# Down projection with seven products for eight in 8 of its 22 contracted tiles, and two modulation blocks summed earlier

## The chip, the cores and the metric

One Trainium2 chip, one of its cores. The time is the device time of the whole program in microseconds (us); below it is the median of several runs. The engines are named as the profile names them: PE (TensorE matmuls), PEld (its weight loads), DVE (VectorE), ACT (ScalarE), POOL (GpSimd), SP (SyncE, which issues most DMAs).

## The reference

One layer of a streaming encoder for 512 + 64 tokens, model width 1024, feed-forward width 2816, all in float32. What matters here is its end, the feed-forward part, and the modulation vectors that feed it:

```python
mod = (jax.nn.silu(c) @ w_ada + b_ada)[:, None, :]
sh1, sc1, gt1, sh2, sc2, gt2 = jnp.split(mod, 6, axis=-1)
...
x = x + gt1 * mixed
h2 = rms_normalize(x) * g_norm_ffn * (1.0 + sc2) + sh2
gate, up = jnp.split(h2 @ w_gate_up, 2, axis=-1)
x = x + gt2 * ((jax.nn.silu(gate) * up) @ w_down)
```

`w_gate_up` is 1024 x 5632, `w_down` 2816 x 1024. `mod` has 6 x 1024 columns, which the kernel makes in 12 blocks of 512; the last two, u = 10 and 11, are `gt2`.

## The kernel before

**Numbers in two parts.** A float32 operand is split into a rounded high part (`...h`, type fp32r, by ACT) and the remainder as low part (`...l`, by DVE: value minus high part). A product is then three matmuls into one PSUM bank: high x high, high x low, low x high. The 576 tokens are two halves of TH = 288; a matmul has a 128 x 128 weight tile and 288 or 290 columns.

**The planner.** The code does not issue instructions. It records them; `Plan.order` then sorts them by a list schedule with durations of its own and a priority for each (the place in the code, moved by `R.prio`: 4000 is earlier, -2000 later), and the chip gets a fixed order for each engine. All instructions therefore carry one line, L573, and are told apart by their tiles.

**Gate and up products.** The hidden dimension has 22 tiles f. For f = 0, 1 four plain products per half are made. From f = 2 on, `STRASSEN` takes a 2 x 2 block scheme with seven products in place of eight: contraction in two halves of four tiles, `g` and `u` as the two column blocks (quadrants `B11`, `B21` in `raw`, `B12`, `B22` in `rawu`), the two token halves as the two row blocks. Operands of the tokens are `A11`, `A12`, `A22` and the sums `S1` to `S4` (tiles `xh...`, `xl...`), those of the weights `B11`, `B21`, `B22` and the sums `T1` to `T4` that DVE makes. The order of the products is 7, 6, 2, 5, then product 1 of the next tile, 3, 4. `prepare` splits the weights of a product into one of six buffers (`wh`, `wl`, three each), six products ahead. Three banks `x`, `y`, `z` collect the products; `evacuate` reads them between the products (tiles `t1`, `u2`, `v`, `gg`, `uu`), and `finish` applies the gate.

**Down projection.** `split_f` splits each finished tile f into `fh`, `fl`: three of them early, 19 at the turn from one projection to the other, mostly in the freed buffers of `A11` to `S4`. Then for each of eight column blocks a the whole contraction runs plainly: 22 tiles x 3 matmuls x 2 halves = 132 matmuls (`fm_in`), then the update of the residual (`x2r`, two DVE instructions per half, 256 and 32 wide), six transposes, copies and stores. For a = 7 the halves run one after the other.

**Modulation blocks 10 and 11.** `ada_columns` makes them during the first columns of the down projection: eight 128 x 512 pieces of `w_ada`, and on DVE for each piece two instructions that multiply it by a per-partition scalar and add it to an accumulator (`aacc`), so 32 for both blocks. Small matmuls with `pick` and a transpose then turn the sums into columns.

Of the kernel before, what the change touches and what calls it, by code (L numbers as in the profile page):

```python
# [13 lines left out]
P = 128  # L14
# [566 lines left out]
def build(tc, I, O):  # L581
# [227 lines left out]

    def ada_out(u, p):  # L810
        ra = adp.tile([P, P], F32, name=f"ra{u}", tag="ra", bufs=2)
        vec.tensor_copy(ra, p[:, 0:P])
        p2 = px(f"padt{u}", "py")
        pe.transpose(p2[:, 0:P], ra, ident)
        vec.tensor_tensor(modc[:, u // 2, 4 * (u % 2):4 * (u % 2) + 4, :],
                          p2[:, 0:P].rearrange("p (g s) -> p g s", g=4)[:, :, 0:2],
                          badc[:, 4 * u:4 * u + 4, None].to_broadcast([P, 4, 2]), OP.add)

    def ada_columns(u, pl, bufs, sums=("aacc0", "aacc1"), raws=None):
# [13 lines left out]
        p = px(f"padc{u}")  # L833
        R.slack = 3.0
        with R.prio(4000):
            for s in range(2):
                for g in range(4):
                    pe.matmul(p[32 * g:32 * g + 32, 0:P], pick[:, s], acc[s][:, P * g:P * g + P], start=(s == 0), stop=(s == 1),
                              tile_position=(0, 32 * g))
            ada_out(u, p)  # L840
        R.slack = SLACK
# [969 lines left out]
    def weight_sum(f, q):

        if (f, q) not in sums:
            b = rawf[f]
            x, y = {"T1": ("B12", "B11"), "T2": ("B22", "T1"), "T3": ("B22", "B12"), "T4": ("B21", "T2")}[q]
            y = b[y] if y in b else weight_sum(f, y)
            t = ffw.tile([P, 4, P], F32, name=f"{q}_{f}", tag=q, bufs=2 if q in ("T1", "T2") else 1)
            vec.tensor_tensor(t, b[x], y, OP.subtract)
# [3 lines left out]
    def prepare():  # L1822
        j = made[0]
        f, q = preps[j]
        pl, tag, bufs = (x2p, "wx", 2) if 6 <= j < NP0 else (wp, ("wh", "wl")[j % 2], NWH)
        wops[f, q] = t = pl.tile([P, 8, P], F32R, name=f"wf{j}", tag=tag, bufs=bufs)
        src = rawf[f][q] if q[0] == "B" else weight_sum(f, q)
        act.activation(t[:, 0:4], src, AF.Copy)
        vec.tensor_tensor(t[:, 4:8], src, t[:, 0:4].bitcast(F32), OP.subtract)
        left[f] -= 1  # L1830
        if left[f] == 0 and f + 2 < NFT:
            load_f(f + 2)
        made[0] += 1

    def product(f, w, x, out, starts):
        w = wops[f, w]
        n = TH if x in ("A21", "A22", "S1", "S3") else TW
        out = out[:, :n]
        for k in range(4):
            xh, xl = xqh[x, k // 2][:, k % 2, :n], xql[x, k // 2][:, k % 2, :n]  # L1840
            for a, m in ((k, xh), (k, xl), (4 + k, xh)):
                pe.matmul(out, w[:, a], m, start=(starts and k == 0 and a < 4 and m is xh), stop=(k == 3 and a == 7),
                          skip_group_check=not starts)

    fe = R.mkpool("fearly", side="right", reuse_waits="tile")
    NEARLY = 3
    fh = [fe.tile([P, T], F32R, name=f"fh{k}") for k in range(NEARLY)]
    fl_ = [fe.tile([P, T], F32R, name=f"fl{k}") for k in range(NEARLY)]
    ev = R.mkpool("evac", side="right", reuse_waits="tile")
    fa, banks, parts = [], {}, {}  # L1850

    def split_f(k):
        act.activation(fh[k], fa[k], AF.Copy)
        vec.tensor_tensor(fl_[k], fa[k], fh[k].bitcast(F32), OP.subtract)

    def part(f, n):
        d = parts.setdefault(f, {})
        if n not in d:
            d[n] = ev.tile([P, 2, TW] if n in ("gg", "uu") else [P, TW], F32, name=f"{n}{f}", tag=n, bufs=2)
        return d[n]  # L1860
# [29 lines left out]
    def bank(f, b):  # L1890
        if (f, b) not in banks:
# [11 lines left out]
    def free_after(j):  # L1903

        return -1 if j < NP0 else N0 // 2 + j - NP0 if j < NP0 + 6 else N0 + j - 6 - NP0

    load_f(0)
    load_f(1)
    for i, (f, w, x, b, starts, *p) in enumerate(steps):
# [11 lines left out]
        else:  # L1921
            with R.prio(4000):
                evacuate(f, p[0])
            if p[0] == 4 and f <= NEARLY + 1:
                split_f(f - 2)
        if i == N0 - 1:
            R.close(x2p)
            gp = R.mkpool("act", side="right", reuse_waits="tile")
            fa += [gp.tile([P, T], F32, name=f"f{k}") for k in range(NFT)]
            for k in range(NPLAIN):  # L1930
                finish(k)
    R.close(ffw)
    down_specs()
    fhl = R.mkpool("fhl", reuse_waits="tile")
    homes = [(q, j) for q in ("A11", "S3", "S2", "A12", "S1", "S4", "A22") for j in range(2)]
    for k in range(NEARLY, NFT):
        for d, n in ((fh, "h"), (fl_, "l")):
            if homes:
                d.append(fp.tile([P, T], F32R, name=f"f{n}{k}", tag=f"x{n}{homes[0][0]}{homes[0][1]}"))
            else:  # L1940
                d.append(fhl.tile([P, T], F32R, name=f"f{n}{k}"))
        homes = homes[1:]
    for k in range(NEARLY, NFT):
        split_f(k)
    R.close(gp, ev)
    adg = R.mkpool("adag", reuse_waits="tile")
    with R.prio(2000):
        for u in (10, 11):
            ada_columns(u, adg, 2)
        vec.tensor_scalar(gt2h, gt2, 0.5, None, op0=OP.mult)  # L1950
    yop = R.mkpool("yout", reuse_waits="tile")
    fd = (lambda k: fh[k], lambda k: fl_[k])
    for a in range(8):
        w = getw()
        xo = yop.tile([P, 2, TH], F32, name=f"x2r{a}", tag="x2r", bufs=3)
        sync.dma_start(xo, x2_d[:, a])
        yo = yop.tile([P, 6, P], F32, name=f"yo{a}", tag="yo", bufs=3)
        pss = [pmm(f"pwd{a}{hf}")[:, 0:1] for hf in range(2)] if a == 7 else None
        ps = None if pss else pmm(f"pwd{a}")
        if a < 7:  # L1960
            fm_in(ps, w, *fd)
        cols = slice(a * P, (a + 1) * P)
        if a < 2:
            c = yop.tile([P, 2, TH], F32, name=f"c{a}", tag="c", bufs=2)
            with R.prio(4000):
                act.activation(c, ps[:, :, :TH], AF.Copy)
            ps = c
        for hf in range(2):
            if a == 7:
                fm_one(pss[hf][:, 0, :TH], w, *fd, hf)  # L1970
            x = xo[:, hf]
            for s, c0, n in SEG:
                vec.scalar_tensor_tensor(x[:, c0:c0 + n], (pss[hf][:, 0] if pss else ps[:, hf])[:, c0:c0 + n], gt2h[:, a, s:s + 1], x[:, c0:c0 + n], op0=OP.mult, op1=OP.add)
            p = px(f"pyt{a}{hf}", ("px", "py")[hf])
            R.slack = 2.0 if a < 2 else SLACK
            for j, (c0, n) in enumerate(BLOCKS):
                pe.transpose(p[:n, j * P:(j + 1) * P], x[:, c0:c0 + n], ident)
            R.slack = SLACK
            act.activation(yo[:, 3 * hf], p[:, :P], AF.Copy)
            vec.tensor_copy(yo[:, 3 * hf + 1], p[:, P:2 * P])  # L1980
            act.activation(yo[:HS, 3 * hf + 2], p[:HS, 2 * P:3 * P], AF.Copy)
            sync.dma_start(O["y_prompt"][0][HP * hf:HP * hf + HP, cols].rearrange("(t p) d -> p t d", p=P), yo[:, 3 * hf:3 * hf + 2])
            (act if a == 7 and hf == 1 else sync).dma_start(O["y_sample"][0][HS * hf:HS * hf + HS, cols], yo[:HS, 3 * hf + 2])
    R.close(yop, adg, fhl, fp, fe, adp, psum, wp, cp)
    R.run()
# [36 lines left out]
```

## Time and profile before

| | |
|---|---|
| median of three runs | 1372.54 us (1371.54 to 1372.80) |
| the profiled execution | 1372.75 us, of it the span 1370.9 us |
| PE busy in the span | 1352.1 us |
| DVE busy | 1071.3 us |
| ACT busy | 722.4 us |
| POOL busy | 223.8 us |
| granted PE clock | 1.00 |
| gate and up products | from about 966 us to 1220 us of the span |
| down projection | from about 1215 us to the end of the span |

A row of instructions gives engine, line, operation, written tile `<-` read tiles, and the shape; buffer numbers are left out, so `T` is any weight sum and `mm`, `px`, `py` are PSUM banks. "Mean ns of one" contains the end of an instruction that overlaps the next; the distance between starts is shorter. A matmul of 288 columns is shown with some 300 ns, but the next starts about 133 ns later. PEclk is the clock that TensorE was granted.

### The profile page before, as it was taken

The page shows a single profiled execution, that of the slowest core. Times are in us where ns is not written, and L with a number is a line of the kernel's source. Part 1 is how long each engine was busy: PE and PEld are TensorE (multiplying, and loading weights), DVE is VectorE, ACT ScalarE, POOL GpSimd, SP SyncE. Part 2 cuts the span into 40 slices and gives each one's busy share as a digit, 9 for nine tenths or more (in the row PEclk, how much of TensorE's full clock was granted, in tenths as well). Part 3 has the DMA queues.
Part 4 walks back from the last instruction along what each step waited for, and adds up shares of the span by engine and source line. Part 5 has one row for each costly group of instructions (what it writes and reads, how often), then busy time and mean ns, then how long its engine had stood idle before and what let it go on. Part 6 is the DMA issues. An engine that isn't in the chain of part 4 may idle for free.

```text
span 1370.9 us, 27495 instructions
## 1 busy us (share of the span) xinstructions
PE 1352.1 (99%) x10711; PEld 1314.6 (96%) x10711; DVE 1071.3 (78%) x2105; ACT 722.4 (53%) x1547; POOL 223.8 (16%) x291
## 2 busy tenths in 40 slices
PE   7999999999999999999999999999999999999998
PEld 5999999999999999999999999999999999999998
DVE  4579998887678779899888688877998888887422
ACT  5454234766777656666566342225666666671221
POOL 2211004230300134454433300000000000000000
PEclk9999999999999999999999999999999999999999
DMA  9542447463763445444446477757233333336431
GB/s 330 161 133 80 110 121 199 93 166 94 184 154 96 113 117 137 100 131 139 138 137 209 126 216 229 242 174 233 73 95 101 97 94 93 93 94 209 143 111 30
DMA packets 252916, 191.68 MB, mean 140 GB/s; under 512 B 24873, under 2 KB 222770, under 8 KB 252786
## 3 DMA queue, kind: packets, MB, share of 16 engines
q1 hardware_dynamic: 249634, 179.36, 44.3%
q0 software_dynamic: 3104, 10.55, 4.1%
q8 instruction: 84, 1.38, 0.4%
q14 instruction: 46, 0.38, 0.1%
q10 hardware_dynamic: 48, 0.02, 0.0%
HBM read 154.57 MB, written 24.84 MB: 131 GB/s over the span
## 4 chain that ended last, share of the span: by engine, by line
PE 52%; ACT 2%; issue 1%; DVE 1%; DMA 1%; POOL 1%; POOLq 0%; DVEq 0%; ACTq 0%
PE mm L573 40%; PE py L573 7%; PE px L573 5%; ACT dec L573 1%; DMA hTl<-o_d 0%; DVE cu L573 0%; ACT decS L573 0%; DMA bc<-acs_d 0%; POOL dec L573 0%; POOL xc L573 0%; ACT bc L573 0%; DVE dec L573 0%; POOL hst L573 0%; DVE xdt L573 0%; DVE xw L573 0%
## 5 line engine op out<-in xcount | busy, mean ns | idle before, releaser
L573 ACT ACTIVATE wh<-raw 128x1024 fp32r<-128x1024 f32 (+1 forms) x159 | 156.2, 986 | 239.5 <-PE mm L573 182.4
L573 PE MATMUL mm<-hTh,wl 128*128 128x288 f32 x1152 | 264.0, 303 | 0.3 <-ACT xc L573 0.3
L573 PE MATMUL mm<-hTl,wh 128*128 128x288 f32 x1152 | 261.1, 302 | 0.0
L573 PE MATMUL mm<-hTh,wh 128*128 128x288 f32 x1152 | 259.8, 302 | 0.2 <-ACT hTh L573 0.2
L573 DVE TENSOR_TENSOR wl<-raw,wh 128x1024 fp32r<-128x1024 f32 (+1 forms) x117 | 141.7, 1213 | 76.7 <-ACT wh L573 76.2
L573 PEld LDWEIGHTS mm<-hTh,wl 128*128 128x128 f32 x1152 | 188.3, 189 | 2.5 <-issue 0.6
L573 PEld LDWEIGHTS mm<-hTl,wh 128*128 128x128 f32 x1152 | 187.6, 189 | 2.0 <-issue 0.4
L573 PEld LDWEIGHTS mm<-hTh,wh 128*128 128x128 f32 x1152 | 186.9, 189 | 2.3 <-ACT hTh L573 0.4
L573 DVE SCALAR_TENSOR_TENSOR cu<-xc,wc,cu 128x579 f32<-128x579 f32 x96 | 92.0, 958 | 2.9 <-ACT cu L573 1.9
L573 PE MATMUL mm<-xhS,wh 128*128 128x290 f32 (+1 forms) x376 | 83.6, 296 | 0.0
L573 PE MATMUL mm<-xhS,wl 128*128 128x288 f32 (+1 forms) x360 | 80.0, 296 | 0.0
L573 DVE SCALAR_TENSOR_TENSOR aacc<-adr,sil,aacc 128x512 f32<-128x512 f32 x98 | 68.4, 746 | 6.7 <-DMA adr<-in_w_ada 6.5
L573 PE MATMUL mm<-wl,hTh 128*128 128x256 f32 x256 | 72.8, 285 | 0.1
L573 PE MATMUL mm<-wh,hTl 128*128 128x256 f32 x256 | 72.6, 284 | 0.0
L573 PE MATMUL mm<-wh,hTh 128*128 128x256 f32 x256 | 72.2, 284 | 0.3 <-ACT wh L573 0.3
L573 PE MATMUL mm<-xlS,wh 128*128 128x288 f32 (+1 forms) x252 | 65.9, 297 | 0.0
L573 PEld LDWEIGHTS mm<-xhS,wh 128*128 128x128 f32 x376 | 62.7, 189 | 0.0
L573 PEld LDWEIGHTS mm<-xhS,wl 128*128 128x128 f32 x360 | 60.1, 189 | 0.0
L573 PE MATMUL mm<-yl,wh 128*128 128x288 f32 x256 | 55.5, 297 | 0.0
L573 PE MATMUL mm<-yh,wl 128*128 128x288 f32 x256 | 55.1, 296 | 0.0
L573 PE MATMUL mm<-yh,wh 128*128 128x288 f32 x256 | 54.8, 296 | 0.0
L573 POOL TENSOR_TENSOR cs<-bc,xb 128x512 f32<-128x512 f32 (+1 forms) x32 | 46.0, 1442 | 45.5 <-ACT bc L573 25.1
(464 smaller groups left out, 3603.0 us busy)
## 6 DMA issues: line engine op xcount, KB each, us to landing
raw<-in_w_in SPq DMA_DIRECT2D x80, 512.0 KB, 4.2
adr<-in_w_ada SPq DMA_DIRECT2D x44, 512.0 KB, 5.0
rawu<-in_w_gate_up SPq DMA_DIRECT2D x22, 512.0 KB, 4.0
raw<-in_w_gate_up SPq DMA_DIRECT2D x22, 512.0 KB, 3.8
wl<-raw POOLq DMA_DIRECT2D x20, 512.0 KB, 4.7
bc<-acs_d SPq DMA_DIRECT2D x32, 256.0 KB, 3.8
raw<-in_w_branch_ssm SPq DMA_DIRECT2D x16, 512.0 KB, 4.4
raw<-in_w_down SPq DMA_DIRECT2D x16, 512.0 KB, 4.3
```

The costliest lines, as they stand in the source:

```text
L573: getattr(engines[x.eng], x.fn)(*[real(a) for a in x.args], **{k: real(v) for k, v in x.kw.items()})
```

## The change

1. **Seven products in the down projection.** The columns are taken in four pairs d: blocks d and d + 4. For contracted tiles 0 to 7 (`KS = 8`) the same seven-product scheme is used, with the tiles 0 to 7 kept in one buffer `fs` whose four quadrants are A11, A12, A21, A22; the sums `S1` to `S4` are made in place, `S1`, `S2` early (`early_sums`, after f = 17). Tiles 8 to 21 stay plain. An output block is updated more than once, as its bank's partial sums become ready (`add_out`).
2. **Splits.** Tiles 8 to 13 are split as they are finished; 14 to 21 are copied by a DMA to their own buffer and split at the turn; `down_operand` splits the seven operands.
3. **Modulation blocks 10 and 11** are summed in the gate and up stage: a quarter of a block after each of the tiles 3 to 6 and 10 to 13 (`ada_part`), with buffers of the weight sums `T1`, `T2` for the pieces, which leaves one of two buffers for those sums meanwhile.
4. **Low parts by DMA.** From f = 3 on the low part of `B22` is no longer a DVE subtraction: ACT writes the negated high part and a DMA issued by POOL adds the raw weight to it. The same is done for the plain weights of tiles 14 to 21 of pair 0.

```diff
+        if d == 0:
+            dsteps += [plain("e", 0, 8, 6, 0, (("y", 0, True), ("z2", 1, True))), plain("e", 1, 8, 6, 1, (("x2", 0, True), ("w", 1, True)))]
+            dsteps += [prod(1, "x"), prod(7, "z"), prod(6, "x"), prod(2, "y"), prod(5, "x"), prod(4, "z"), prod(3, "x")]
+            dsteps += [plain("l", 0, 14, 8, 0, (("y", 0, False), ("z", 1, False))), plain("l", 1, 14, 8, 1, (("x", 0, False), ("w", 1, False)))]
...
+        else:
+            dsteps += [prod(1, "x"), prod(7, "z"), prod(6, "x"), prod(2, "y")]
+            dsteps += [plain(0, j, k0, nk, 0, (("y", 0, False), ("z", 1, False))) for j, (k0, nk) in enumerate(((8, 6), (14, 8)))]
+            dsteps += [prod(5, "x"), prod(4, "z"), prod(3, "x")]
...
             act.activation(t[:, 0:4], src, AF.Copy)
+            if q == BY_DMA and f in range(NPLAIN + 1, NFT):
+                act.activation(t[:, 4:8], t[:, 0:4].bitcast(F32), AF.Copy, scale=-1.0)
+                pool.dma_start(t[:, 4:8], src, accum_op=OP.add)
+            else:
+                vec.tensor_tensor(t[:, 4:8], src, t[:, 0:4].bitcast(F32), OP.subtract)
...
+    def early_sums():
+        down_x["S2"] = gs.tile([P, 4, TH], F32, name="s2", tag="s2")
+        with R.prio(-2000):
+            vec.tensor_tensor(quad(0, 1), quad(0, 1), quad(4, 1), OP.add)
+            vec.tensor_tensor(down_x["S2"], quad(0, 1), quad(0, 0), OP.subtract)
...
+    def ada_part(u, n):
+        if n == 0:
+            accs[u] = gs.tile([P, 2, 512], F32, name=f"aacc{u}", tag="s2")
+        with R.prio(-2000):
+            for k in (2 * n, 2 * n + 1):
+                raw = ffw.tile([P, 512], F32, name=f"wada{u}_{k}", tag=("T1", "T2")[k % 2], bufs=2)
+                sync.dma_start(raw, w_ada[P * k:P * k + P, 512 * u:512 * u + 512])
+                for j in range(2):
+                    a = accs[u][:, j]
+                    if k == 0:
+                        vec.tensor_scalar(a, raw, sil[:, k, j:j + 1], None, op0=OP.mult)
+                    else:
+                        vec.scalar_tensor_tensor(a, raw, sil[:, k, j:j + 1], a, op0=OP.mult, op1=OP.add)
...
+            if p[0] == 4 and f == 17:
+                early_sums()
+            if p[0] == 4 and f in range(3, 17):
+                u, n = 10 + (f - 3) // 7, (f - 3) % 7
+                if n < 4:
+                    ada_part(u, n)
+                if n == 6 and u < 12:
+                    ada_end(f, u)
...
+    down_operand("A11")
+    vec.tensor_tensor(quad(0, 0), quad(4, 1), down_x["S2"], OP.subtract)
+    down_x["S3"] = quad(0, 0)
+    for q in ("S3", "S2", "A12"):
+        down_operand(q)
...
+        if what == "product":
+            p, z = t
+            product(("s", d), PRODS[p][0], PRODS[p][1], bk[z], p in (1, 7) or p == 2 and d > 0)
             with R.prio(4000):
-                act.activation(c, ps[:, :, :TH], AF.Copy)
...
+                if p in (1, 6):
+                    add_out(a, int(p == 6), bk["x"])
+                if p in (5, 7):
+                    add_out(b, 1, bk[z])
+                if p == 4 and d > 0:
+                    add_out(a, 1, bk["z"])
```

The order of the instructions, at three places. First DVE in the gate and up stage, a stretch in the middle of it. `wh`, `wl` are weight buffers that get their low part, `T_0_10307` to `T_1_10312` the buffers of the weight sums, `gg`, `uu` the gate and up tiles, `f` a finished tile. Before:

```order
L573 TENSOR_TENSOR wh_100<-T_0_10309,wh_100 128x512
L573 TENSOR_TENSOR wl_103<-raw_97,wl_103 128x512
L573 TENSOR_TENSOR gg_10941<-u_1_10947,py_109 128x288
L573 TENSOR_TENSOR wh_101<-rawu_10313,wh_101 128x512
L573 TENSOR_TENSOR wl_104<-T_0_10308,wl_104 128x512
L573 SCALAR_TENSOR_TENSOR gg_10941<-f_0_11225,gg_10941 128x2x288
L573 TENSOR_TENSOR T_0_10308<-raw_97,T_1_10312 128x512
L573 SCALAR_TENSOR_TENSOR f_0_11225<-uu_10943,gg_10941 128x2x256
L573 SCALAR_TENSOR_TENSOR f_0_11225<-uu_10943,gg_10941 128x2x32
```

Now, where the second group of modulation sums begins (`s_0_11235` is their accumulator, `sil` the scalars; here the buffers `T_0_10309` and `T_0_10311` hold pieces of `w_ada`):

```order
L573 TENSOR_SCALAR s_0_11235<-T_0_10309,sil_117 128x512
L573 TENSOR_TENSOR f_0_11218<-gg_10941,fh_0_10932 128x576
L573 TENSOR_TENSOR uu_10942<-v_10948,py_108 128x288
L573 TENSOR_TENSOR wh_101<-raw_97,wh_101 128x512
L573 TENSOR_SCALAR s_0_11235<-T_0_10309,sil_117 128x512
L573 TENSOR_TENSOR wl_104<-T_1_10310,wl_104 128x512
L573 SCALAR_TENSOR_TENSOR s_0_11235<-T_0_10311,sil_117,s_0_11235 128x512
L573 TENSOR_TENSOR T_0_10307<-rawu_10313 128x512
L573 TENSOR_TENSOR wh_99<-raw_98,wh_99 128x512
L573 TENSOR_TENSOR gg_10940<-u_0_10946,py_108 128x288
L573 TENSOR_TENSOR T_1_10310<-rawu_10313,raw_98 128x512
L573 SCALAR_TENSOR_TENSOR s_0_11235<-T_0_10311,sil_117,s_0_11235 128x512
```

The sums stand singly between the low parts and the reads of PSUM, an early split (`f_0_11218`) has come in, and the row that read `rawu` for a low part is gone.

Second, ACT at the preparation of B22 near the stage's end. Before:

```order
L573 ACTIVATE uu_10943<-mm_113 128x290
L573 ACTIVATE wl_104<-raw_97 128x512
L573 ACTIVATE wh_99<-rawu_10313 128x512
L573 ACTIVATE gg_10941<-gg_10941 128x2x256
L573 ACTIVATE gg_10941<-gg_10941 128x2x32
```

Now:

```order
L573 ACTIVATE uu_10943<-mm_113 128x290
L573 ACTIVATE wl_102<-raw_97 128x512
L573 ACTIVATE wh_100<-rawu_10313 128x512
L573 ACTIVATE wh_100<-wh_100 128x512
L573 ACTIVATE gg_10941<-gg_10941 128x2x256
```

The negated copy follows the high part at once; POOL, which has nothing else in this stage, then issues the adding DMA.

Third, DVE at the turn. Before, between the last gate and up products, splits of finished tiles into the freed operand buffers (`xlS`, `xlA`) and weights of the down projection (`wl<-raw`):

```order
L573 TENSOR_TENSOR xlS_0_10297<-f_0_11225,xhS_0_10296 128x576
L573 TENSOR_TENSOR xlS_0_10299<-f_0_11226,xhS_0_10298 128x576
L573 TENSOR_TENSOR xlA_0_10281<-f_0_11227,xhA_0_10280 128x576
L573 TENSOR_TENSOR xlA_0_10283<-f_0_11228,xhA_0_10282 128x576
L573 TENSOR_TENSOR gg_10941<-u_1_10947,py_109 128x288
L573 TENSOR_TENSOR wl_104<-raw_98,wh_101 128x768
```

Now, during the seven products of pair 0 (`mm_112` is the bank of `x` and `y`, `mm_113` that of `z`; `gg`, `uu` here hold output blocks 0 and 4):

```order
L573 SCALAR_TENSOR_TENSOR gg_10940<-mm_112,gt2h_91,gg_10940 128x256
L573 SCALAR_TENSOR_TENSOR gg_10940<-mm_112,gt2h_91,gg_10940 128x32
L573 TENSOR_TENSOR wh_101<-rawu_10314,wh_101 128x512
L573 TENSOR_TENSOR xlS_0_10301<-fs_11234,xhS_0_10300 128x576
L573 SCALAR_TENSOR_TENSOR uu_10942<-mm_113,gt2h_91,uu_10942 128x256
L573 SCALAR_TENSOR_TENSOR uu_10942<-mm_113,gt2h_91,uu_10942 128x32
L573 TENSOR_TENSOR xlS_0_10303<-fs_11234,xhS_0_10302 128x576
L573 SCALAR_TENSOR_TENSOR gg_10940<-mm_112,gt2h_91,gg_10940 128x256
L573 SCALAR_TENSOR_TENSOR gg_10940<-mm_112,gt2h_91,gg_10940 128x32
L573 TENSOR_TENSOR xlA_0_10289<-fs_11234,xhA_0_10288 128x576
```

The updates of the outputs, which read the banks that the next products write, stand between the splits of the operands that later products need.

More of the change, by code (lines that the diff above doesn't have):

```diff
@@ L1802, in build @@
+    last_use = {}
+    for i, (f, *_) in enumerate(steps[N0:]):
+        last_use[NP0 + i] = N0 + i
+    for i, t in enumerate(dsteps):
+        if t[1] == "product":
+            keys = [(("s", t[0]), PRODS[t[2]][0])]
+        else:
+            keys = [((t[2], t[0]), (t[3], n)) for n in "hl"]
+        for key in keys:
+            if key not in preps:
+                preps.append(key)
+            last_use[preps.index(key)] = len(steps) + i
     assert NRAW == 2 and NPLAIN == 2
     def load_f(f):
+        if f not in range(NFT):
+            kind, d = f
+            parts_ = {"s": [(0, 8, d), (0, 8, d + 4)], "e": [(8, 6, d), (8, 6, d + 4)], "l": [(14, 8, d), (14, 8, d + 4)],
+                      0: [(8, 6, d), (14, 8, d)], 1: [(8, 6, d + 4), (14, 8, d + 4)]}[kind]
+            t = []
+            for (r0, nk, a), pl, tag in zip(parts_, (wp, ffw), ("raw", "rawu")):
+                t.append(pl.tile([P, nk, P], F32, name=f"{tag}d{kind}{d}", tag=tag, bufs=2))
+                sync.dma_start(t[-1], kview(w_dn[P * r0:P * (r0 + nk), P * a:P * a + P]))
+            rawf[f] = {"B11": t[0][:, 0:4], "B21": t[0][:, 4:8], "B12": t[1][:, 0:4], "B22": t[1][:, 4:8]} if kind == "s" else t
+            return
@@ L1816, in weight_sum @@
             y = b[y] if y in b else weight_sum(f, y)
-            t = ffw.tile([P, 4, P], F32, name=f"{q}_{f}", tag=q, bufs=2 if q in ("T1", "T2") else 1)
+            t = ffw.tile([P, 4, P], F32, name=f"{q}_{f}" if f in range(NFT) else f"{q}_d{f[1]}", tag=q, bufs=2 if q in ("T1", "T2") else 1)
             vec.tensor_tensor(t, b[x], y, OP.subtract)
@@ L1836, in product @@
         w = wops[f, w]
-        n = TH if x in ("A21", "A22", "S1", "S3") else TW
+        n = TH if x in ("A21", "A22", "S1", "S3") or f not in range(NFT) else TW
         out = out[:, :n]
@@ L1841, in product, with split_f @@
             for a, m in ((k, xh), (k, xl), (4 + k, xh)):
-                pe.matmul(out, w[:, a], m, start=(starts and k == 0 and a < 4 and m is xh), stop=(k == 3 and a == 7),
+                pe.matmul(out, w[:, a, :], m, start=(starts and k == 0 and a < 4 and m is xh), stop=(k == 3 and a == 7),
                           skip_group_check=not starts)
     fe = R.mkpool("fearly", side="right", reuse_waits="tile")
-    NEARLY = 3
-    fh = [fe.tile([P, T], F32R, name=f"fh{k}") for k in range(NEARLY)]
-    fl_ = [fe.tile([P, T], F32R, name=f"fl{k}") for k in range(NEARLY)]
+    KS, NEARLY = 8, 6
+    fh = {k: fe.tile([P, T], F32R, name=f"fh{k}") for k in range(KS, KS + NEARLY)}
+    fl_ = {}
     ev = R.mkpool("evac", side="right", reuse_waits="tile")
[L1850 to L1854, printed above, removed]
+    fa, banks, parts = {}, {}, {}
+    def split_f(k, src):
+        act.activation(fh[k][:, :, :TH], src, AF.Copy)
+        vec.tensor_tensor(t2(fl_[k]), src, fh[k][:, :, :TH].bitcast(F32), OP.subtract)
     def part(f, n):
@@ L1858, in part @@
         if n not in d:
-            d[n] = ev.tile([P, 2, TW] if n in ("gg", "uu") else [P, TW], F32, name=f"{n}{f}", tag=n, bufs=2)
+            d[n] = ev.tile([P, 2, TW] if n in ("gg", "uu") else [P, TW], F32, name=f"{n}{f}", tag=n, bufs=1 if n == "v" else 2)
         return d[n]
@@ L1928, in build @@
             gp = R.mkpool("act", side="right", reuse_waits="tile")
-            fa += [gp.tile([P, T], F32, name=f"f{k}") for k in range(NFT)]
+            gs = R.mkpool("acts", side="right", reuse_waits="tile")
+            fs = gs.tile([P, KS, T], F32, name="fs")
+            fa.update({k: fs[:, k, :] for k in range(KS)})
             for k in range(NPLAIN):
                 finish(k)
[L1932 to L1964, printed above, removed]
-            with R.prio(4000):
-                act.activation(c, ps[:, :, :TH], AF.Copy)
[L1967 to L1983, printed above, removed]
@@ L1984, in build, with down_operand @@
-    R.close(yop, adg, fhl, fp, fe, adp, psum, wp, cp)
+    vec.tensor_scalar(gt2h, gt2, 0.5, None, op0=OP.mult)
+    def down_operand(q):
+        src = down_x[q]
+        with R.prio(URGENT):
+          for j in range(2):
+            for e, n in ((xqh, "h"), (xql, "l")):
+                e[q, j] = fp.tile([P, 2, TH], F32R, name=f"d{n}{q}{j}", tag=f"x{n}{q}{j}")
+            act.activation(xqh[q, j], src[:, 2 * j:2 * j + 2], AF.Copy)
+            vec.tensor_tensor(xql[q, j], src[:, 2 * j:2 * j + 2], xqh[q, j].bitcast(F32), OP.subtract)
@@ new lines, in build @@
+    URGENT = 0
+    down_operand("A11")
[3 more added lines that the diff above has]
+        down_operand(q)
+    vec.tensor_tensor(quad(4, 0), quad(4, 0), down_x["S2"], OP.subtract)
+    down_x["S4"] = quad(4, 0)
+    for q in ("S1", "A22", "S4"):
+        down_operand(q)
+    R.close(gs)
+    fhl = R.mkpool("fhl", side="right", reuse_waits="tile")
+    for k in range(KS + NEARLY, NFT):
+        fh[k] = fhl.tile([P, 2, TW], F32R, name=f"fh{k}")
+        split_f(k, t2(fl_[k].bitcast(F32)))
+        fh[k] = fh[k][:, :, :TH]
@@ new lines, in open_pair @@
+    def open_pair(d):
+        for c, tag in ((d, "gg"), (d + 4, "uu")):
+            xo[c] = ev.tile([P, 2, TH], F32, name=f"x2r{c}", tag=tag, bufs=2)
+            sync.dma_start(xo[c], x2_d[:, c])
+        m = pmm(f"pd{d}")
+        bk = {"x": m[:, 0, :TH], "y": m[:, 1, :TH], "w": m[:, 1, :TH]}
+        if d == 0:
+            m = pmm("pdb")
+            bk["z"], bk["x2"] = m[:, 0, :TH], m[:, 1, :TH]
+            bk["z2"], bk["w"] = px("pdz2")[:, :TH], px("pdw")[:, :TH]
+        else:
+            bk["z"] = px(f"pdz{d}")[:, :TH]
+        return bk
@@ new lines, in build @@
+    seen = set()
+    for i, (d, what, *t) in enumerate(dsteps):
+        a, b = d, d + 4
+        if d not in seen:
+            seen.add(d)
+            bk = open_pair(d)
+        with R.prio(4000):
+            while made[0] < len(preps) and len(steps) + i > free_after(made[0]):
+                prepare()
+        if what == "product":
+            p, z = t
+            product(("s", d), PRODS[p][0], PRODS[p][1], bk[z], p in (1, 7) or p == 2 and d > 0)
+            with R.prio(4000):
+                if p in (1, 6):
[4 more added lines that the diff above has]
+                    add_out(a, 1, bk["z"])
+            if p == 4 and d > 0:
+                put_out(a, 1)
+            continue
+        g, slot, k0, nk, c, on = t
+        w = {n: wops[(g, d), (slot, n)] for n in "hl"}
+        for k in range(nk):
+            f = k0 + k
+            for n, r in (("h", fh), ("h", fl_), ("l", fh)):
+                for z, hf, starts in on:
+                    starts = starts and k0 == 8
+                    pe.matmul(bk[z], w[n][:, k, :], r[f][:, hf, :] if len(r[f].shape) > 2 else r[f][:, hf * TH:(hf + 1) * TH],
+                              start=starts and k == 0 and n == "h" and r is fh, stop=(k == nk - 1 and n == "l"),
+                              skip_group_check=not (starts and g == "e"))
+        for z, hf, starts in on:
+            e = (a, b)[c]
+            if g == "e" and z in ("x2", "z2") or k0 == 14 and not (c == 0 and z == "z" and d > 0):
+                with R.prio(4000):
+                    add_out(e, hf, bk[z])
+                if k0 == 14:
+                    put_out(e, hf)
@@ L1985, in build @@
+    R.close(yop, fhl, ffw, gp, ev, fp, fe, adp, psum, wp, cp)
     R.run()
```

99 lines of the change are left out of this document (81 added, 18 removed).

## The prediction, made before the changed kernel was run

> **What bounds the kernel now.** I read the page first, for the engine that fills the span, then the chain that ended last through the down projection and the tail.
>
> ```profile
> span 1370.9 us, 27495 instructions
> PE 1352.1 (99%) x10711; PEld 1314.6 (96%) x10711; DVE 1071.3 (78%) x2105; ACT 722.4 (53%) x1547; POOL 223.8 (16%) x291
> ```
>
> ```profile
> 1313.76 16.32 PE mm L573 x123
> 1330.07 0.33 PE px L573 x3
> 1330.40 0.27 PE mm L573 x2
> 1330.67 0.22 PE py L573 x2
> 1330.88 0.93 PE mm L573 x7
> 1331.82 0.11 PE py L573
> 1331.93 16.31 PE mm L573 x123
> ...
> 1358.15 7.69 PE mm L573 x58
> 1365.84 0.02 issue
> 1365.86 0.49 DVE x2r L573
> 1366.35 0.04 issue
> 1366.40 0.57 PE py L573 x3
> ```
>
> TensorE (PE) is busy 99% of the span. In the chain each row begins where the row before it ends, and between 1313.76 and 1331.93 there is PE alone: one column block of the down projection, 123 + 2 + 7 = 132 matmuls and 6 transposes, with no wait. So a matmul taken out here is worth its issue interval, 16.32/123 = 0.1327 us, as long as nothing new makes PE wait. The last rows show how fast a result is handed over: DVE starts 0.02 us after the last matmul's row, PE 0.04 us after DVE.
>
> Next I ask whether the stage that receives work, the feed-forward products, is bound by PE as well. Three stretches of 11.25 us, the time of one tile f there:
>
> ```profile
> core 0: us, PE busy (x) PEld busy (x) DVE busy (x) ACT busy (x) POOL busy (x), PEclk, DMA share, GB/s
> 1000.00:1011.25 11.25, 11.25 (x85) 11.18 (x85) 11.18 (x20) 7.75 (x15) 0.00 (x0) 1.00 0.20 57
> 1011.25:1022.50 11.25, 11.25 (x85) 11.18 (x85) 11.15 (x22) 9.07 (x19) 0.00 (x0) 1.00 0.43 124
> 1100.00:1111.25 11.25, 11.25 (x87) 11.25 (x86) 9.64 (x18) 7.16 (x15) 0.00 (x0) 1.00 0.31 92
> ```
>
> PE is full at a granted clock of 1.00 in all three. VectorE (DVE) has 9.64 of 11.25 us in the steady state, and in the first two 11.18 and 11.15, 99%, without a gap on PE. A full DVE alone does not stop PE; a DVE that falls behind by more than its lead does.
>
> **The change, part by part.**
>
> *Removed matmuls.* Per pair of column blocks, 8 contracted tiles cost 8 x 3 x 2 x 2 = 96 matmuls before and 7 x 12 = 84 after. Four pairs: 48 fewer. The other 14 tiles, the 48 transposes and the matmuls that pick out the modulation's columns are as many as before. 48 x 0.1327 = -6.4 us, all on the path, since nothing else lies on it there.
>
> *Sums of the last two modulation blocks.* Their 32 DVE instructions move from the down projection, where DVE has room, into eight tiles f (3 to 6, 10 to 13), four per tile. The prices are start-to-start times:
>
> ```profile
> 1252.90 2.74 DVE L573 SCALAR_TENSOR_TENSOR aacc<-adr,sil,aacc 128x512 f32<-128x512 f32 x4
> ...
> 1228.40 3.43 DVE L573 TENSOR_TENSOR fl<-f,fh 128x576 fp32r<-128x576 f32 x5
> ...
> 1274.77 2.33 DVE L573 SCALAR_TENSOR_TENSOR x2r<-c,gt2h,x2r 128x256 f32<-128x256 f32 x8
> ```
>
> ```profile
> 1170.12 0.69 DVE L573 TENSOR_TENSOR wh<-T,wh 128x512 fp32r<-128x512 f32 x1
> 1170.72 0.69 DVE L573 TENSOR_TENSOR T<-rawu 128x512 f32<-128x512 f32 x1
> 1171.33 0.45 DVE L573 TENSOR_TENSOR uu<-v,py 128x288 f32<-128x288 f32 x1
> 1171.69 0.69 DVE L573 TENSOR_TENSOR wl<-raw,wl 128x512 fp32r<-128x512 f32 x1
> ```
>
> A sum costs 2.74/4 = 0.68, a split's low part 3.43/5 = 0.69, an output update (a 256 and a 32 wide piece) 2.33/4 = 0.58, a weight's low part or sum 0.61, a 288 wide read of PSUM 0.36. Per f: +4 x 0.68 = 2.72; -0.61, because the low part of B22 goes to a DMA; about +0.1 for the gating in two halves from f = 8 on (2 x 0.36 against 0.67). First group: 9.64 - 0.61 + 2.72 = 11.75, 0.5 over the 11.25 each, 2.0 behind after four tiles, recovered in the three after them (9.03 each). Second group, with one early split each (+0.69): 9.64 - 0.61 + 0.1 + 0.69 + 2.72 = 12.54, 1.3 over, 5.2 behind after four tiles. What covers it is the lead of the weights:
>
> ```profile
> 1164.09 0.63 ACT L573 ACTIVATE wl<-rawu 128x512 fp32r<-128x512 f32 x1 [0.53 <-PE py L573]
> ```
>
> ```profile
> 1164.76 0.69 DVE L573 TENSOR_TENSOR wl<-rawu,wl 128x512 fp32r<-128x512 f32 x1
> ```
>
> ```profile
> 1162.60 3.19 PE py L573 x24
> ...
> 1169.01 4.84 PE mm L573 x36
> ```
>
> This is B22 of one tile. Its buffer comes free when the first 12 of the 24 matmuls end (1162.60 + 1.6 = 1164.2), its low part is done at 1165.45, and the product that reads it is the last third of the 36 (1169.01 + 24/36 x 4.84 = 1172.24), its low rows two matmuls later, 1172.5. The lead is 7.0 us, more than 5.2. Behind a sum in DVE's queue stand low parts with that lead and PSUM reads whose banks alternate by tile; its own load (256 KB) can be late:
>
> ```profile
> T<-in_w_ada SPq DMA_DIRECT2D x8, 256.0 KB, 4.6
> ```
>
> These are 16 loads on SP's queue, against 8 of double size in the down projection before; also new on it are eight copies of finished tiles from SBUF to SBUF, of the size of these rows:
>
> ```profile
> gate_d<-sg SPq DMA_DIRECT2D x16, 288.0 KB, 2.3
> ```
>
> Both stand ahead of weight loads, which are asked for a whole tile (11.25 us) ahead. Bounds of the part: 0 if the lead covers everything, 2.0 + 5.2 = 7.2 if every microsecond shows. I take 0.7, near the lower end, since the two 99% rows are the nearest case.
>
> *Low part of B22 by DMA, 19 tiles.* ACT makes a negated copy (0.63, so 7.16 + 0.63 of 11.25 on ACT, free) and POOL issues an adding DMA of 256 KB. POOL is idle there (0.00). Nearest rows, twice the size, in an earlier stage:
>
> ```profile
> L573 POOL DMA_DIRECT2D wl<-raw x20: 850/864/960, 201.6 to 414.1; - x20
> ...
> DMA to landing us min/median/max: 4.5/4.7/7.2
> ...
> DVE  4579998887678779899888688877998888887422
> ```
>
> High part done 1164.72, copy 1165.35, landing 4.7 later 1170.05, needed 1172.5: 2.4 to spare at the median, nothing at the maximum. Cost taken 0; bounds 0 and, at 7.2 every time, 19 x 0.05 = 1. The raw tile is read longer, so its reload starts some 4.6 us later, inside the tile of lead named above.
>
> The Trainium skill speaks against this part: "SBUF — State Buffer", section "SBUF: two separate sides", says that a DMA issued from POOL starves while DVE runs an operation in a 2-port mode, and gives 620 ns alone against some 3100 ns overlapped. By the page the landing would be about 2.5 longer (an estimate from those two figures), 7.2, just in time, and the sum the same. The rows lean against more: the 20 DMAs lay between 201.6 and 414.1 us, slices 6 to 13 of 40 in the row above, where DVE is at 6 to 9 tenths, and 4.7 is their median.
>
> *The turn to the down projection.* Before, 19 tiles were split there; now it is 14 operand splits, two wide sums (1.3 each, estimated from 0.69 for half the width), and 8 more splits afterwards. From the first freed operand, product (21, 1), to the last of the seven products of pair 0, PE has nine products, 72 plain matmuls and six products: 15 x 1.61 + 72 x 0.1327 = 33.7 us. DVE has in that stretch 14 weight pieces of 512 (8.5), two of 768 (1.8), 14 splits (9.7), two wide sums (2.6), five PSUM reads (1.8), two gatings (3.2) and six output updates (3.5): 31.1. 2.6 us are left. Queued behind each other are the reads of bank x: product 6 overwrites what the update after product 1 reads, product 3 what the update after 5 reads. Bounds 0 and 3 (the spare gone and as much again); I take 0.8, since DVE is at 92% and late by about half an instruction at such a point.
>
> *Hand-overs in pairs 1 to 3.* After product 1, DVE has one product's time, 1.61 us, for 0.58 of update and 0.06 of hand-over, with at worst a 1.2 us weight piece ahead. The next pair opens on the other double bank. Taken 0.3; bounds 0 and 12 x 0.64 = 7.7 if all twelve updates of the four pairs that hold a bank were bare.
>
> *Tail.* It has the same last update, transposes and stores: 0.
>
> Sum: -6.4 + 0.7 + 0 + 0.8 + 0.3 = -4.6. The profiled execution took 1372.75 (span 1370.9 and 1.85 around it); that gives 1368.15. The median is 1372.54, 0.2 lower, so the median after should be 1367.9.
>
> **The rivals.**
>
> *DVE becomes the bound in the feed-forward stage.* For it: 12.54 of work in 11.25. Against it: the 7.0 us lead and the two full rows. If all 7.2 show instead of 0.7: 1367.9 + 6.5 = 1374.4, no measurable change.
>
> *The DMA's low part arrives late (slower).* Place: product 3 of every f from 3 on. It decides where the mean landing passes 7.15 us; from there each further microsecond costs 19. At 8.0 it is 0.85 x 19 = 16, so 1384; to undo the gain of 4.6 and reach +2.7 it takes 7.3/19 = 0.4 late. For it: DVE is denser than beside the 20 DMAs, and one of those took 7.2. Against it: half the bytes, an idle POOL, a median of 4.7. By the page of the skill named above, a landing longer than that would need several 2-port operations in a row, and no run here shows one.
>
> *The turn and the hand-overs are bare.* 3 + 7.7 instead of 1.1: 1367.9 + 9.6 = 1377.5 at the most; half of it, 1372.7, no change. Against it: the tail's hand-over of 0.02 and 0.04.
>
> That the change does not do what it says is excluded: the instruction lists hold 48 matmuls fewer.
>
> **How the numbers follow.** A difference below 0.2%, 2.7 us, can't be told from none. The forecast (stalls under 3.7 us in all): 0.72. Full DVE: 0.11. Late DMA: 0.08. Bare turn and hand-overs: 0.09. Faster takes the forecast and a little of the rivals' lower ends, 0.73; slower takes the DMA and the upper end of the others, 0.11; same, 0.16. Lower end of the range: no stall at all, 1372.54 - 6.4 = 1366.1, and 0.3 for the spread of the runs: 1365.8. Upper end: half of the full-DVE price and half of the turn on top of the forecast, near 1374. The forecast's own range is 1366 to 1369.8.
>
> **What would show it.** Right: a pair of column blocks in 252 x 0.1327 + 12 x 0.11 = 34.8 us without a row of another engine in the chain, where two columns took 36.3; a chain of PE alone from f = 3 to 21; low parts from POOL landing in under 5 us. Wrong: rows of DVE in the chain at f = 10 to 14 (first rival), PE waiting for a POOL DMA once per 11.25 us (second), PE waiting for the updates of the outputs between products 1 and 6 (third).

## The result and the profile after

The changed kernel takes 1381.36 us (median of six runs, 1380.37 to 1384.87); the kernel before, on the same chip, 1372.82 (six runs, 1371.54 to 1373.51). The ratio is 1.0066, with a 95% interval of 1.0053 to 1.0079: slower by 8.5 us. Forecast were 1367.9, and 1374.0 as the upper end of the range, so both the time and the sign are wrong. The profiled execution took 1381.94, with a span of 1380.2 and a granted clock of 0.999, as good as before.

The page of the changed kernel, span and busy times:

```profile
span 1380.2 us, 27675 instructions
PE 1351.5 (98%) x10663; PEld 1308.6 (95%) x10663; DVE 1096.2 (79%) x2180; ACT 745.7 (54%) x1606; POOL 240.5 (17%) x312
```

There are 48 PE instructions fewer (10663 against 10711), as the change says, yet PE is busy for almost as long in a longer span. So something makes PE stop. The view of waits, for PE from 960 us on (each row: PE's work, what released it, idle us in total, times, the longest):

```profile
PE mm L573 <- DVE gg L573: 8.0, 18, 0.7
PE mm L573 <- DVE uu L573: 0.9, 2, 0.6
PE py L573 <- DVE uu L573: 0.7, 1, 0.7
PE mm L573 <- DMA wl<-rawu: 0.3, 1, 0.3
```

`gg` and `uu` are here the tiles that hold the residual in the down projection, so the writer is an output update (`add_out`). Matmuls wait for updates twenty times. In the kernel before, the same view has one row only, that of the tail (the third one here, with another name for the residual):

```profile
PE py L573 <- DVE x2r L573: 0.6, 1, 0.6
```

The waits come two by two, ten pairs, all after 1231 us. One of them in the timeline, PE first, then DVE (start, duration, and in brackets how long the engine was idle and who released it):

```profile
1303.06 0.30 PE L573 MATMUL mm<-xhS,wh 128*128 128x288 f32 x1
1303.19 0.30 PE L573 MATMUL mm<-xhA,wl 128*128 128x288 f32 x1
1303.33 0.29 PE L573 MATMUL mm<-xlA,wl 128*128 128x288 f32 x1
1303.46 0.29 PE L573 MATMUL mm<-xhA,wl 128*128 128x288 f32 x1
1304.33 0.40 PE L573 MATMUL mm<-xhA,wl 128*128 128x288 f32 x1 [0.58 <-DVE gg L573]
1304.57 0.29 PE L573 MATMUL mm<-xlA,wl 128*128 128x288 f32 x1
1304.70 0.29 PE L573 MATMUL mm<-xhA,wl 128*128 128x288 f32 x1
1305.34 0.40 PE L573 MATMUL mm<-xhA,wl 128*128 128x288 f32 x1 [0.34 <-DVE gg L573]
```

```profile
1303.79 0.48 DVE L573 SCALAR_TENSOR_TENSOR gg<-mm,gt2h,gg 128x256 f32<-128x256 f32 x1 [0.21 <-PE mm L573]
1305.03 0.25 DVE L573 SCALAR_TENSOR_TENSOR gg<-mm,gt2h,gg 128x32 f32<-128x32 f32 x1 [0.76 <-PE mm L573]
```

At 1303.06 product 6 (operand `xhS`) issues its last matmul into accumulator x. Product 2 (`xhA`) goes on into y. After three of its matmuls PE stops, DVE does the 256 columns of the update of x, PE does three more, and DVE, idle for 0.76 us, waits for these three before it does the other 32 columns, for which PE waits once more. From start to start 1303.46 to 1304.33 is 0.87 where 0.133 would do, and 1304.70 to 1305.34 is 0.64: 0.74 + 0.50 lost, and some 0.1 after each restart (0.24 instead of 0.133 to the next start). Yet no matmul of product 2 touches what DVE reads: x is one bank, y another. What x and y do share is the two-bank buffer that one call of `pmm` allocates (`m[:, 0]` and `m[:, 1]`). The emitted program, PE's order with its waits, in pair 0 (x and y are both `mm_112` there):

```
L573 MATMUL mm_112<-xhS_0_10298,wh_99 128x288
L573 MATMUL mm_112<-xhA_0_10280,wl_102 128x288
L573 MATMUL mm_112<-xlA_0_10281,wl_102 128x288
L573 MATMUL mm_112<-xhA_0_10280,wl_102 128x288
L573 MATMUL mm_112<-xhA_0_10280,wl_102 128x288 [waits DVE_49]
L573 MATMUL mm_112<-xlA_0_10281,wl_102 128x288
L573 MATMUL mm_112<-xhA_0_10280,wl_102 128x288
L573 MATMUL mm_112<-xhA_0_10282,wl_102 128x288 [waits DVE_49]
```

and DVE's of the same update:

```
L573 SCALAR_TENSOR_TENSOR gg_10940<-mm_112,gt2h_91,gg_10940 128x256 [waits PE_49]
L573 SCALAR_TENSOR_TENSOR gg_10940<-mm_112,gt2h_91,gg_10940 128x32 [waits PE_49]
```

The waits stand in the program in both directions, in the middle of a product and between the two pieces of an update. The kernel's planner does not count them: `View.box` in its code treats each 512 columns of PSUM as a thing of its own, so it mixes the pieces of the update with the matmuls as if both could run at once.

The feed-forward stage, where the prediction feared for DVE, is as full as it said, and PE does not stop:

```profile
1100.00:1111.25 11.25, 11.25 (x86) 11.25 (x85) 11.25 (x22) 8.24 (x19) 0.86 (x2) 1.00 0.63 162
1111.25:1122.50 11.25, 11.25 (x86) 11.25 (x85) 11.12 (x21) 8.24 (x19) 0.86 (x2) 1.00 0.54 142
1122.50:1133.75 11.25, 11.25 (x86) 11.25 (x85) 11.25 (x22) 8.24 (x19) 0.86 (x2) 1.00 0.55 144
```

(window, then busy us of PE, PEld, DVE, ACT, POOL). The low parts by DMA, from the view of DMAs (size, median us from issue to landing):

```profile
wh<-rawu POOLq DMA_DIRECT2D x10, 256.0 KB, 3.3
wl<-rawu POOLq DMA_DIRECT2D x9, 256.0 KB, 3.3
```

### The profile page after: what moved, and what is told of

The parts are those of the page before. It is cut to its first block, busy times and chain, and to the rows that moved or that the text cites. A ratio compares the mean times of both kernels' runs of the same rounds, so it can differ in the third digit from the quotient of the medians.

```text
span 1380.2 us, 27675 instructions
## 1 busy us (share of the span) xinstructions
PE 1351.5 (98%) x10663; PEld 1308.6 (95%) x10663; DVE 1096.2 (79%) x2180; ACT 745.7 (54%) x1606; POOL 240.5 (17%) x312
## 4 chain that ended last, share of the span: by engine, by line
PE 47%; issue 5%; DVE 2%; ACT 1%; DMA 1%; POOL 1%; POOLq 0%; DVEq 0%; ACTq 0%
PE mm L573 35%; PE px L573 6%; PE py L573 6%; ACT dec L573 1%; DVE gg L573 1%; DMA hTl<-o_d 0%; DMA wl<-rawu 0%; DVE cu L573 0%; DMA bc<-acs_d 0%; POOL dec L573 0%; POOL xc L573 0%; ACT decS L573 0%; ACT bc L573 0%; DVE dec L573 0%; POOL r L573 0%
## 5 line engine op out<-in xcount | busy, mean ns | idle before, releaser
L573 ACT ACTIVATE wh<-raw 128x1024 fp32r<-128x1024 f32 (+2 forms) x143 | 138.4, 972 | 163.3 <-PE mm L573 114.0
L573 DVE TENSOR_TENSOR wl<-raw,wh 128x1024 fp32r<-128x1024 f32 (+1 forms) x97 | 118.4, 1224 | 40.4 <-ACT wh L573 32.2
L573 PE MATMUL mm<-xhS,wh 128*128 128x290 f32 (+1 forms) x296 | 65.9, 297 | 0.1
L573 PE MATMUL mm<-xhS,wl 128*128 128x290 f32 (+1 forms) x288 | 64.0, 297 | 0.3 <-DMA wl<-rawu 0.3
L573 DVE SCALAR_TENSOR_TENSOR aacc<-adr,sil,aacc 128x512 f32<-128x512 f32 x70 | 49.0, 746 | 5.9 <-DMA adr<-in_w_ada 5.9
L573 ACT ACTIVATE dec<-dec,nacs 128x128 f32<-128x128 f32 x128 | 41.8, 396 | 21.2 <-POOL dec L573 21.1
L573 ACT ACTIVATE P<-lg,mn 128x128 f32<-128x128 f32 (+4 forms) x72 | 41.8, 581 | 18.9 <-DVE mn L573 18.8
L573 PEld LDWEIGHTS mm<-xhS,wh 128*128 128x128 f32 x296 | 49.8, 189 | 0.5 <-DVE modc L573 0.3
```

What stands on the lines that cost most here:

```text
L573: getattr(engines[x.eng], x.fn)(*[real(a) for a in x.args], **{k: real(v) for k, v in x.kw.items()})
```

## The experiments

Theory 1: the stalls come from the shared two-bank buffer, whose halves are ordered against each other. Theory 2: DVE is full at the turn and the updates are late. Theory 3: an update between two products costs its own length wherever its bank is.

**The accumulators laid out otherwise.** In `open_pair`, no bank that is read by an update shares a buffer with one that is written meanwhile:

```diff
         m = pmm(f"pd{d}")
-        bk = {"x": m[:, 0, :TH], "y": m[:, 1, :TH], "w": m[:, 1, :TH]}
         if d == 0:
-            m = pmm("pdb")
-            bk["z"], bk["x2"] = m[:, 0, :TH], m[:, 1, :TH]
-            bk["z2"], bk["w"] = px("pdz2")[:, :TH], px("pdw")[:, :TH]
+            n = pmm("pdb")
+            bk = {"y": m[:, 0, :TH], "z2": m[:, 1, :TH], "x": n[:, 0, :TH], "w": n[:, 1, :TH]}
+            bk["x2"], bk["z"] = px("pdx2")[:, :TH], px("pdz")[:, :TH]
         else:
-            bk["z"] = px(f"pdz{d}")[:, :TH]
+            bk = {"x": m[:, 0, :TH], "y": px(f"pdy{d}")[:, :TH]}
+            bk["w"], bk["z"] = bk["y"], px(f"pdz{d}")[:, :TH]
```

> The changed kernel with the seven accumulators of the down projection laid out otherwise: no bank that an update reads shares a two-bank buffer with a bank that the products beside it write. Matmuls, updates, weights and their numbers are the same. Theory 1, the two halves of one two-bank buffer are ordered against each other by the emitted waits, and the ten stalls of two hand-overs each (about 0.74 + 0.50 us) come from that: all ten go, 1381.4 - 12.4 = 1369, 1367.5 to 1371. Theory 2, DVE is late there because it is full: the stalls stay wherever the bank is, 1379 to 1382. Theory 3, any update that comes between two products costs its own length, since an accumulation is handed over with no cover: the stalls move to other rows, 1377 or more.

Measured: 1367.96 us (1367.51 to 1370.65), 0.9973 of the kernel before (0.9963 to 0.9983), so 13.4 below the changed kernel. The page, and PE's waits from 960 us on:

```profile
span 1366.1 us, 27682 instructions
PE 1346.1 (99%) x10663; PEld 1308.1 (96%) x10663; DVE 1093.7 (80%) x2180; ACT 745.3 (55%) x1606; POOL 242.0 (18%) x312
```

```profile
PE mm L573 <- DVE f L573: 1.0, 1, 1.0
PE py L573 <- DVE uu L573: 0.7, 1, 0.7
PE mm L573 <- DMA wl<-rawu: 0.3, 1, 0.3
```

All twenty waits are gone, with the same instructions on DVE (2180). Theories 2 and 3 fall: the same updates by the same full DVE no longer stop PE. In the emitted program the 32-wide piece of that update has lost its wait for PE. The chain gives the length of a pair, from product 7 (z, `px`) of one pair to product 7 of the next:

```profile
1293.36 1.59 PE px L573 x12
...
1328.14 1.59 PE px L573 x12
```

34.78 us; in the changed kernel the same stretch is longer by two stalled updates:

```profile
1300.17 1.59 PE px L573 x12
...
1337.89 1.59 PE px L573 x12
```

37.72. The prediction's count for a pair was 34.8.

**An update in one piece.**

```diff
-        for s, c0, n in SEG:
-            vec.scalar_tensor_tensor(x[:, c0:c0 + n], src[:, c0:c0 + n], gt2h[:, a, s:s + 1], x[:, c0:c0 + n], ...)
+        vec.scalar_tensor_tensor(x, src, gt2h[:, a, 0:1], x, op0=OP.mult, op1=OP.add)
```

> The changed kernel, but an output update is one DVE instruction over 288 columns instead of one of 256 and one of 32; it leaves out the second modulation segment (the 32 sample columns take the first segment's gate). Banks as in the changed kernel. Theory 1: each stall has one hand-over instead of two, so ten times about 0.50 us go, 1381.4 - 5 = 1376.5, 1375 to 1378. Theory 2, DVE is late because it is full: it is relieved by 32 instructions of 0.25, 8 us in all, most of them where it has room, so the change is under 1.5 us unless the stalls go altogether.

Measured: 1376.20 us (1375.70 to 1376.48). PE's waits from 960 us on:

```profile
PE mm L573 <- DVE gg L573: 5.4, 9, 0.6
PE mm L573 <- DVE uu L573: 0.6, 1, 0.6
```

Ten waits instead of twenty, each for the whole update, and 5.2 us less by the medians, as theory 1 expected: the second hand-over of the pair is paid for the 32 columns alone.

**The low part of B22 on DVE again.**

```diff
-    BY_DMA, DMA_LOW = "B22", ("l",)
+    BY_DMA, DMA_LOW = "", ("l",)
```

> The changed kernel with the low part of B22 subtracted by DVE again in the feed-forward stage (19 instructions of 0.61 us more on DVE, 19 adding transfers of 256 KB fewer, 19 copies fewer on ACT). Banks as in the changed kernel. Theory 1 (stalls by shared two-bank buffers) says nothing of this: 1381 plus what the fuller DVE shows. If DVE is the bound in the tiles with sums, 8 x 0.61 = 4.9 us more show: 1386. If its lead covers this too: within 1 us of 1381.4. If late adding transfers had cost time, it would be faster: 1375 or less.

Measured: 1382.82 us (1381.94 to 1383.55), 1.0076 of before (1.0062 to 1.0090) against 1.0066 (1.0053 to 1.0079) for the changed kernel. PE's waits:

```profile
PE mm L573 <- DVE gg L573: 8.0, 18, 0.7
PE mm L573 <- DVE uu L573: 0.9, 2, 0.6
PE mm L573 <- DVE ra L573: 0.7, 1, 0.7
```

The twenty stalls are untouched, and one wait of 0.7 us is new in the feed-forward stage. The medians differ by 1.5, a little more than the 1 us expected if the lead covers all, and far from the 4.9 of a DVE that bounds the stage. So DVE's lead covers 0.61 us more per tile nearly whole, and the adding transfers had cost nothing that shows here (the one wait of 0.3 us for them is gone). Whether the DMA saves anything at all can't be told: the intervals overlap.

**Sharing in one pair of four.** With the new layout, y goes back into the half beside x in pair 2 alone:

```diff
-            bk = {"x": m[:, 0, :TH], "y": px(f"pdy{d}")[:, :TH]}
+            bk = {"x": m[:, 0, :TH], "y": m[:, 1, :TH] if d == 2 else px(f"pdy{d}")[:, :TH]}
```

> The kernel with the banks laid out otherwise, but in pair 2 of the four pairs alone x and y share a two-bank buffer again. Theory 1: two of the ten stalls come back, at the update of the first column block's second half beside product 2 and at its first half beside product 5, about 2 x 1.24 = 2.5 us above the kernel with no sharing. Theories 2 and 3: no difference between the two.

Measured: 1371.38 us (1369.66 to 1372.57), by the medians 3.4 above the layout without sharing, on the same chip; by the ratios to the kernel before (0.9992 against 0.9973) 2.6. The view of waits has four again, and the chain shows them in pair 2:

```profile
PE mm L573 <- DVE gg L573: 1.8, 4, 0.6
```

```profile
1297.98 0.49 DVE gg L573
1298.52 0.68 PE mm L573 x3
1299.22 0.26 DVE gg L573
...
1313.27 0.68 PE mm L573 x3
1313.94 0.02 issue
1313.97 0.26 DVE gg L573
```

Two stalled updates, at the two places named, come back with the shared buffer: the cause is shown. Their size by the timeline's arithmetic is 2.5, and 2.9 by the length of a pair above (37.72 against 34.78), which has the slow restarts in it; the expectation of 2.5 left these out.

**The same two accumulators in two one-bank buffers.** This tells the buffer from the banks.

```diff
+            if d == 2:
+                bk["x"], bk["z"] = bk["z"], bk["x"]
```

> The kernel with the banks laid out otherwise, but in pair 2 x and y stand in the two one-bank buffers of the tag px and z in one half of a two-bank buffer: the same updates beside the same products as in the kernel where pair 2 shares, only that the two banks are two buffers. Theory 1, the order is that of the buffer: no stall in pair 2, the same time as without sharing, 1368 (within 1 us). Rival, DVE's read of one bank and PE's writes to the next bank disturb each other whatever the buffers, or the update comes too late there: two stalls of two hand-overs return, 2.5 to 3.4 us more.

Measured: 1368.03 us (1367.38 to 1369.53), 0.9970 of before (0.9959 to 0.9981), and PE waits for the same three things as without sharing. The update of x and the matmuls of product 2 into y, DVE and then PE:

```profile
1297.74 0.64 DVE L573 SCALAR_TENSOR_TENSOR gg<-px,gt2h,gg 128x256 f32<-128x256 f32 x2
```

```profile
1297.44 0.29 PE L573 MATMUL px<-xhA,wl 128*128 128x288 f32 x1
1297.57 0.30 PE L573 MATMUL px<-xlA,wl 128*128 128x288 f32 x1
1297.70 0.43 PE L573 MATMUL px<-xhA,wl 128*128 128x288 f32 x2
1297.96 0.30 PE L573 MATMUL px<-xlA,wl 128*128 128x288 f32 x1
1298.10 0.43 PE L573 MATMUL px<-xhA,wl 128*128 128x288 f32 x2
```

DVE reads one bank from 1297.74 on, both pieces without a break, while PE writes another with a start every 0.13 us. So it is neither the update, nor its lateness, nor the reading of a bank while another is written: it is the buffer that holds both. The Trainium skill, "PSUM — Partial Sum Buffer", section "Terms", bars two engines from the same bank at the same time. These rows, with two engines in two banks at once, agree, and the order in the changed kernel is one that its program added.

**What the sums cost in the feed-forward stage.** With the new layout, 24 of the 32 sums left out:

```diff
                 for j in range(2):
                     a = accs[u][:, j]
+                    if k not in (0, 7):
+                        continue
```

> The kernel with the banks laid out otherwise, with 24 of the 32 sums of the last two modulation blocks left out (row blocks 1 to 6; the loads of all eight stay, so the modulation of two blocks is incomplete). It measures what the sums in the feed-forward stage cost. If DVE's lead hides them: within 1 us of 1368. If each microsecond by which they overfill the tiles shows: 24 x 0.68 = 16.3 us of work less, of which up to 7.2 came off the path: 1361.

Measured: 1366.39 us (1366.00 to 1366.84), beside a kernel before of 1371.26 on that chip: 0.9956 (0.9939 to 0.9973). By the medians 4.9 below before, against 4.4 with all sums, so 0.5 for 24 sums; by the ratios 2.3, with intervals that overlap. PE waits for the same three things as with all sums, none of them DVE in the feed-forward stage. The second expectation, 1361, is out.

**The sums done twice.**

```diff
                         vec.scalar_tensor_tensor(a, raw, sil[:, k, j:j + 1], a, op0=OP.mult, op1=OP.add)
+                    vec.scalar_tensor_tensor(a, raw, sil[:, k, j:j + 1], a, op0=OP.mult, op1=OP.add)
```

> The kernel with the banks laid out otherwise, with each of the 32 sums done twice (the second adds the same term again). Eight tiles get 8 x 0.68 = 5.44 us of sums each. By the prediction's count: first group 9.64 - 0.61 + 5.44 = 14.5, 3.2 over 11.25, 12.9 behind after four tiles; second group 15.3, 4.0 over, 16 behind. With a lead of 7.0 us, 5.9 + 9.0 = 15 us show: 1383, 1378 to 1388. If the lead were far larger, or the counts too high, under 5: 1370. If there were no lead and the single sums just fit: 13 + 16 = 29: 1397.

Measured: 1386.88 us (1385.78 to 1389.49), 1.0108 of before (1.0091 to 1.0124). Some of PE's waits between 1060 and 1200 us, which were absent with single sums:

```profile
PE mm L573 <- ACT wh L573: 4.8, 2, 2.9
...
PE mm L573 <- DVE wh L573: 1.5, 1, 1.5
PE mm L573 <- DVE s L573: 1.5, 1, 1.5
```

Against the new layout with single sums that is 1.0108 - 0.9973 = 1.35% or 18.5 us, at the upper edge of what was expected. But not all of it is waiting. PE's waits in this stretch add up to 11.8 us, where single sums have none. The mean granted clock was 0.992 to 0.995 in the four executions, against 0.999 or 1.000 with single sums, and the view of windows shows where: 0.50 from 1084 to 1088 and from 1176 to 1180 us, each time after long waits (PE stood for 1.96 and 1.54 us shortly before the first). Matmuls start 0.24 us apart there instead of 0.133; no run here isolates what lowers the clock:

```profile
1085.19 0.44 PE L573 MATMUL mm<-xlS,wh 128*128 128x288 f32 x1
1085.43 0.68 PE L573 MATMUL mm<-xhS,wh 128*128 128x288 f32 x2
1085.91 0.44 PE L573 MATMUL mm<-xlS,wh 128*128 128x288 f32 x1
```

By the same count (12.9 + 16 = 28.9 us behind) 17.1 were covered if only the waits are charged to DVE, and 10.4 if the slow clock is charged to it too: an estimate of 5 to 9 us of lead for each group. With single sums the second group falls 5.2 behind, near the lower end.

**The best version again.**

> The kernel with the banks laid out otherwise once more, beside the one above on the same chip, and as the best version: 0.997 of the kernel before, 1368.

Measured: 1368.51 us (1367.46 to 1371.40), 0.9973 of before (0.9964 to 0.9983), the same ratio on another occasion. The layout without sharing beats both kernels.

## Why the prediction was wrong

*The step that failed* is the term "Hand-overs in pairs 1 to 3", taken as 0.3 and bounded by 12 x 0.64 = 7.7 for the updates of all four pairs. The ten stalls together measured 13.4, the difference between the two layouts; eight of the ten lie in pairs 1 to 3, two in pair 0. Two things were wrong in the term. First, which work waits for an update: only true overwrites were counted (product 6 on x after product 1), each with 1.61 us of cover. The waits that cost time were between a reader of one half and the matmuls into the other half of the same buffer, which have no cover at all, since the order puts them side by side. That "the next pair opens on the other double bank" was beside the point; the partners stood in the same pair. Second, the price. The bound took a bare update at 0.58 plus 0.06, the 0.06 from the gaps of 0.02 and 0.04 around DVE in the tail. In the view of waits above, that same tail hand-over stops PE for 0.6 us, and the matmul before a hand-over counts with its whole 0.29 us instead of the 0.133 to the next start. An update in two pieces, with PE's matmuls in between, is two round trips: 0.74 + 0.50 and the restarts, 13.4/10 = 1.3 each. So the bound itself was too low, and with it the range and the rival of "bare turn and hand-overs" (1377.5 at the most). That rival had the right stage and the right sort of wait, PE for the updates. It did not have the mechanism, nor for the most part the place: in pair 2, say, PE does not wait between products 1 and 6, but in products 2 and 5. Its chance of 0.09 was far too little. The waits stand in the emitted order of the changed kernel, in the middle of a product, and the prediction did not go by them. (The upper end of the range is by its own working 1367.9 + 3.6 + 1.5 = 1373.0 and not 1374; the measured time is above both.)

*Removed matmuls, -6.4: right.* With the stalls gone, PE is busy 1346.1 us against 1352.1, 6.0 less, and a pair takes 34.78 us where 34.8 was worked out.

*Sums in the feed-forward stage, +0.7: not contradicted.* Without 24 of the 32 sums the gain is 0.5 by the medians and 2.3 by the ratios, whose intervals overlap, and PE has no wait for DVE there. DVE is full at 11.12 to 11.25 of 11.25 and PE with it, as in the two rows from which the term was taken. The lead, put at 7.0, lies within the 5 to 9 that the doubled sums give.

*Low part by DMA, 0: right.* The landing is 3.3 us at the median, for half the bytes of the rows with 4.7; PE waited for it once, 0.3 us. The Trainium skill, "SBUF — State Buffer", section "SBUF: two separate sides", warns that such a DMA starves beside DVE's 2-port operations. That is not tested here: DVE is full in those tiles, but each of its operations from 1100 to 1133.75 us is a TENSOR_TENSOR or a SCALAR_TENSOR_TENSOR that reads two tensors, and no run shows one of them in a 2-port mode.

*Turn, +0.8: right in size with the new layout, by luck.* There PE has one wait of 1.0 us, for a split (`f`) that stands behind four weight pieces in DVE's queue. The prediction had put the cost at the reads of bank x, and in the kernel that was forecast two of the ten stalls lie in pair 0 instead.

*Tail, 0: right.* The wait for the last update is 0.7 us, the same in all versions.

With the failed term at nothing instead of 0.3 the forecast would have been 1367.6; the layout without sharing measured 1367.96 and 1368.51. The sum described that kernel, and not the one that was forecast.

## What to carry to other kernels

Accumulators that are read while others are written belong in buffers of their own: a buffer that spans two banks was one thing to the waits in this program, though the code only ever takes halves of it and its own planner counts them apart. When an update moves from the end of a buffer's work to the middle of it, read the emitted order for waits within a product before costing the hand-over, and cost each piece of the update as a round trip. And a bound that assumes one wait per update is no bound when an update has two instructions.

## What the runs showed of the hardware

A DVE that is busy for 11.12 to 11.25 of 11.25 us in three tiles running made PE wait nowhere in them; with 5.44 us of sums in each of eight tiles instead of 2.72, the run was 18.5 us longer, 11.8 of it waits of PE. After waits of 1.96 and 1.54 us close together the granted clock was 0.50 for some 4 us at least, with matmul starts 0.24 us apart; after the shorter stalls of the changed kernel (0.7 at most) it stayed at 1.00. One hand-over in mid-product costs more than the instruction waited for: 0.74 us for an update of 0.48 and 0.50 for one of 0.25, with a start after each that comes 0.1 us late.
